# Turning mixing weights and normed head outputs by DMA transposes through memory instead of TensorE transposes

## The chip, the cores and the metric

The kernel runs on one core of one Trainium2 chip. The metric is the device time of one execution in microseconds (us), as a median of several runs. A profile of one execution gives, for the same program, the start and the duration of each instruction on each engine: TensorE (PE, its weight loads listed as PEld), VectorE (DVE), ScalarE (ACT), GpSimd (POOL) and SyncE (SP). POOL, SP and ACT also issue DMAs; all DMAs run on the core's 16 DMA engines.

## The reference, cut to what matters

A two-layer backbone over 256 latent and 256 context tokens with model width 1024, so 512 tokens in all. Layer 0 mixes tokens with a bidirectional mLSTM of 4 heads (256 for q and k, 512 for v), layer 1 with latent attention; a gated convolutional FFN follows each. The change lies in the mLSTM mixer. The recurrence is written in the reference as a chunked scan:

```
wmat = jnp.exp(dmat - mj[..., None]) * jnp.einsum("bhjd,bhsd->bhjs", qc, kc)
num  = g[..., None] * jnp.einsum("bhjd,bhde->bhje", qc, C) + jnp.einsum("bhjs,bhse->bhje", wmat, vc)
h    = num / jnp.maximum(jnp.abs(den), jnp.exp(-mj))[..., None]
...
o    = jax.nn.sigmoid(h_in @ w_og).reshape(Bq, T, M_HEADS, M_DV)
hsum = o * s.transpose(0, 2, 1, 3).astype(h_in.dtype)
return _head_rms_norm(hsum, norm_g) @ w_out
```

For each head and direction a token j thus takes a weighted sum of the values of the tokens s that it may see, divided by the row's own sum; the two directions are added, the result is gated by `o`, normed per token and head, scaled by a gain per column and multiplied by `w_out` (2048 x 1024).

## The kernel before, in words

All matrix products work on f32 numbers that are split into a high part and a low remainder (`split`, lines 443 to 445: ACT copies the high part, DVE subtracts for the low one), and each product is three matmuls (`mm3`, lines 424 to 434: high by high at L430, high by low at L433, low by high at L434). A weight block of 128 x 1024 comes by a DMA on SP's queue (L308) into a ring of raw buffers, is cast by ACT (L345) and subtracted by DVE (L368), and lies in one of three `w` buffers until PE has used it. `Stream` runs up to 8 blocks ahead, as far as buffers are free.

The mLSTM is not run as a scan: for each head the whole 512-token matrix of mixing weights is built, and multiplied with the values. Tokens lie in four tiles of 128 rows, t = 0 and 1 context, t = 2 and 3 latent. Context rows see columns 0 to 255, latent rows columns 0 to 511. The stages for head h are:

- `w_qk(h)`: q and k of head h by 8 chunks of 24 matmuls on one weight block each (L430, L433, L434, named `qk`). After each chunk `tick(2)` puts two steps of the generators in `k.bg` into the program, first the first generator's steps until it is used up, then the next one's. This is how the head before is worked on beside these matmuls: `post(h-2)`, then `head(h-1)`. Ahead of chunk 7 `v_load(h-1)` is put in: four loads of values (`vr`, L1133) and four of output gates (`oh`, L1139) on POOL's queue.
- `head(h-1)`: ACT makes the exponentials, DVE multiplies them by the scores S and normalises, in three groups g: context tiles 0 and 1 together, tile 2, tile 3; the last DVE instruction of a group is L1105. What comes out is rows of mixing weights, tokens j on partitions. The product with the values needs them the other way round, so TensorE turns the 12 blocks of 128 x 128 that are not masked (L1118, twelve `PT<-ident,W` in three PSUM tiles), and ACT and DVE split them from PSUM (L444, L445).
- `av(h-1)`: 36 matmuls of mixing weights by values; DVE multiplies the result by the gate into the tiles `oh` (L1178).
- `s_mm(h)`: scores of head h.
- `post(h-2)`: ACT squares and sums each of the four `oh` tiles (L1188), DVE scales them (L1192), TensorE turns them by 16 transposes of 128 x 128 (L1198, `hnT<-ident,oh`), and ACT and DVE read PSUM, apply the gain per column (which after turning is one number per partition) and split (L1205, L1206) into `hn[4h]` to `hn[4h+3]`.

After `w_qk(3)`, `av(2)` and `s_mm(3)` comes the product with `w_out` (`outmm("mout", ...)`, PE rows named `y`, one weight block and 12 matmuls for each of 16 steps i, of which step i needs `hn[i]`), first for the context tokens. Steps 0 to 7 run with `k.bg = [head(3), post(2)]`, then `av(3)`, then steps 8 to 11, which need `hn[8]` to `hn[11]` of head 2, beside `post(3)`, then steps 12 to 15. Head 3's own transposes stay on TensorE after the change too (`big`, `last`).

Names that matter for space: tag `s2`, 15 buffers of 128 x 512 f32 that nearly all small tiles of these stages share; tag `u`, 31 buffers of 128 x 1024 for split operands. A tile's buffer is given on when the last instruction that touches the tile is done, and a later tile with that tag waits for one. The order of instructions on each engine is made by the framework's scheduler: program order is the priority, and an instruction whose inputs are late lets later ones past it when the program is built, not when it runs. On the chip each queue is worked off strictly in that order.

Of the kernel before, what the change touches and what calls it, by code (L numbers as in the profile page):

```python
# [7 lines left out]
F32 = mybir.dt.float32  # L8
F32R = mybir.dt.float32r
I32 = mybir.dt.int32  # L10
AF = mybir.ActivationFunctionType
ALU = mybir.AluOpType
AX = mybir.AxisListType
# [20 lines left out]
NB, NRAW, NU, NS = 3, 3, 31, 15  # L34
# [366 lines left out]
class K:  # L401
# [41 lines left out]
    def split(self, hi, lo, src):  # L443
        self.nc.scalar.copy(hi, src)  # L444
        self.nc.vector.tensor_sub(lo, src, hi)  # L445

    def smc(self, name):
        o, n = self.off[name]
# [590 lines left out]
        return S  # L1039

    def head(self, h, S, big=False):
        nc = self.nc
        aB = [self.s2("aB0"), self.s2("aB1")]
        for d in range(2):
            nc.gpsimd.dma_start(aB[d], self.ad[d, h:h + 1, :].to_broadcast([128, 512]))
        if not big:
            self.t4_step(2)
        Am = [self.s2("Am0"), self.s2("Am1")]
        for d in range(2):
            nc.vector.tensor_tensor(Am[d].rearrange("p (t s) -> p t s", t=4),  # L1050
                                    aB[d].rearrange("p (t s) -> p t s", t=4),
                                    self.mask[:, d:d + 1, :].to_broadcast([128, 4, 128]), op=ALU.add)
        yield
        full = {0: [(0, 0), (0, 128), (0, 256), (0, 384)], 1: [(128, 256), (0, 0), (0, 256), (0, 256)]}
        P = []
        for g in range(3):
            jbs = [0, 1] if g == 0 else [g + 1]
            if big:
                w = self.uf("W")
                W = [w[:, 0:512], w[:, 512:1024]]  # L1060
            else:
                W = [self.s2("W0"), self.s2("W1")]
            den = self.tiny(4, "den")
            nd = len(jbs)
            rng = {}
            for i, t in enumerate(jbs):
                base = 256 * i if g == 0 else 0
                for d in range(2):
                    o = W[d]
                    bias = self.gcol[:, 0, t, 32 * d + h:32 * d + h + 1]  # L1070
                    spans = [(t * 128, (t + 1) * 128, Am[d])]
                    if d == 0:
                        if t > 0:
                            spans.append((0, t * 128, aB[d]))
                        lo, hi = 0, (t + 1) * 128
                    else:
                        if t == 0:
                            spans.append((128, 256, aB[d]))
                        if t >= 2:
                            spans.append((0, 256, aB[d]))  # L1080
                        if t == 2:
                            spans.append((384, 512, aB[d]))
                        lo, hi = {0: (0, 256), 1: (128, 256), 2: (0, 512), 3: (0, 512)}[t]
                    if d == 1 and t == 3:
                        nc.vector.memset(o[:, 256:384], 0.0)
                    for s0, s1, src in spans:
                        nc.scalar.activation(o[:, base + s0:base + s1], src[:, s0:s1], AF.Exp, bias=bias, scale=1.0)
                    nc.vector.scalar_tensor_tensor(o[:, base + lo:base + hi], o[:, base + lo:base + hi], 1.0,
                                                   S[g][:, base + lo:base + hi], op0=ALU.mult, op1=ALU.mult,
                                                   accum_out=den[:, 2 * i + d:2 * i + d + 1])  # L1090
                    rng[i, d] = (base + lo, base + hi)
            dv = den[:, 0:2 * nd]
            R = self.tiny(4, "R")
            nc.vector.scalar_tensor_tensor(R[:, 0:2 * nd], dv, -1.0, dv, op0=ALU.mult, op1=ALU.max)
            e = self.gcol[:, 1, jbs[0]:jbs[-1] + 1, h::32]
            nc.vector.tensor_tensor(R[:, 0:2 * nd].rearrange("p (t d) -> p t d", d=2),
                                    R[:, 0:2 * nd].rearrange("p (t d) -> p t d", d=2), e, op=ALU.max)
            nc.vector.reciprocal(R[:, 0:2 * nd], R[:, 0:2 * nd])
            for i, t in enumerate(jbs):
                big = {0: 1, 1: 0, 2: 1, 3: 0}[t]  # L1100
                b0, b1 = rng[i, big]
                s0, s1 = rng[i, 1 - big]
                nc.vector.tensor_scalar(W[big][:, b0:b1], W[big][:, b0:b1], R[:, 2 * i + big:2 * i + big + 1], None,
                                        op0=ALU.mult)
                nc.vector.scalar_tensor_tensor(W[big][:, s0:s1], W[1 - big][:, s0:s1],  # L1105
                                               R[:, 2 * i + 1 - big:2 * i + 2 - big], W[big][:, s0:s1],
                                               op0=ALU.mult, op1=ALU.add)
                P.append((W[big], b0))
            yield
        yield  # L1110
        self.PT = []
        for grp in ([(t, s) for s in range(2) for t in (0, 1)], [(t, s) for s in range(2) for t in (2, 3)],
                    [(t, s) for s in (2, 3) for t in (2, 3)]):
            pt = self.ps("PT")
            lead = None
            for n, (t, s) in sorted(enumerate(grp), key=lambda x: -x[1][0] * (x[1][0] > 1)):
                src, b0 = P[t]
                q = nc.tensor.transpose(pt[:, n * 128:(n + 1) * 128], src[:, b0 + s * 128:b0 + (s + 1) * 128], self.ident)  # L1118
                if lead is None:
                    lead = q  # L1120
                elif t > 1:
                    self.behind(q, [lead])
            u = self.u("PT")
            self.split(u[:, 0], u[:, 1], pt)
            self.PT.append(u)
        yield
# [53 lines left out]
        self.PT = self.vh = self.oh = None  # L1180
        return r

    def post(self, h, tt):
        nc = self.nc
        ss = self.tiny(4, "ss")
        jk = self.s2("jk")
# [4 lines left out]
        for t in range(4):  # L1191
            nc.vector.tensor_scalar(tt[t], tt[t], ss[:, t:t + 1], None, op0=ALU.mult)  # L1192
        yield
        g = self.smc("mng")
        for e in range(4):
            pt = self.ps("hnT")
# [6 lines left out]
            k = h * 4 + e  # L1203
            u = self.u("hn")
            nc.scalar.activation(u[:, 0], pt, AF.Copy, scale=g[:, k:k + 1])  # L1205
            nc.vector.scalar_tensor_tensor(u[:, 1], pt, g[:, k:k + 1], u[:, 0], op0=ALU.mult, op1=ALU.subtract)  # L1206
            self.hn[k] = u
        yield


    def bcast(self, row, name):
# [970 lines left out]
def build(tc, off, a, out):  # L2182
    es = ExitStack()
    with es:
# [14 lines left out]
        k.bg2.append(k.ada_all([(0, 3, 4, 8)] + [(l, c, 0, 8) for l, c in ((0, 4), (0, 5), (1, 0), (1, 1), (1, 2), (1, 3), (1, 4), (1, 5))]))  # L2199
        S = None  # L2200
        tt = None
        k.hn = {}
        for h in range(H0):
            gens = []
            if h == 0:
# [2 lines left out]
                gens.append(k.post(h - 2, tt))  # L2208
            if h >= 1:
                gens.append(k.head(h - 1, S))  # L2210
            k.bg = gens
            k.w_qk(h, 2, (lambda: k.v_load(h - 1)) if h >= 1 else None)
            k.drain()
# [3 lines left out]
        k.xc = None  # L2217
        hn = lambda i: (k.hn[i][:, 0], k.hn[i][:, 1])
        pc = k.acc4()
        k.bg = [k.head(3, S, True), k.post(2, tt)]  # L2220
        vs = k.v_steps(3)
        for i in range(8):
            k.outmm("mout", range(i, i + 1), hn, pc, 0, 16, 2, n2=ADA_M)
            next(vs, None)
        k.drain()
        tt = k.av(3)
        k.bg = [k.post(3, tt)]
        k.outmm("mout", range(8, 12), hn, pc, 0, 16, 1, n2=ADA_M)
        k.drain()
        tokr = a["tok"].rearrange("(t p) d -> t p d", p=128)  # L2230
# [132 lines left out]
```

## Time and profile before

| what | value |
|---|---|
| median of 3 runs | 1346.94 us (1346.42 to 1347.75) |
| span of the profiled execution, first to last instruction | 1345.3 us |
| median minus that span (the page gives no other time of the profiled execution) | 1.6 us |
| VectorE busy | 1059.0 us (79%) |
| ScalarE busy | 711.7 us (53%) |
| GpSimd busy | 141.5 us (11%) |
| moved by DMA | 304.02 MB, mean 226 GB/s |

Starts are given in us from the span's start. "busy (x)" in a table of stages is busy time and number of instructions in that stretch. A row of the timeline has start, duration, engine, line, operation, output and inputs, shape, and a count where equal neighbours were merged. A matmul's duration is its whole way through the array; the next one starts before it has ended, so what a matmul costs is read from the distance of starts. DMA issues are listed with the queue that issues them, size, and the median time from issue to landing.

### The profile page before, as it was taken

What the parts mean: (1) busy time and instruction counts of PE and PEld (TensorE: products, weight loads), DVE (VectorE), ACT (ScalarE), POOL (GpSimd) and SP (SyncE); (2) the same over time, 40 slices, a digit from 0 to 9 for tenths busy, and PEclk for the clock granted to TensorE, in tenths of its full rate; (3) what the DMA queues carried; (4) which work ended last, traced back from release to release, by engine and by line L of the source; (5) the groups of instructions that cost most, each with busy time, mean ns of one, the idle gap of its engine ahead of it and who ended that gap; (6) DMA issues with size and microseconds to landing.
All of it is one profiled execution on the core that took longest, in us unless ns stands there. A gap on an engine that the chain in (4) does not pass through costs nothing.

```text
span 1345.3 us, 18750 instructions
## 1 busy us (share of the span) xinstructions
PE 1334.9 (99%) x6659; PEld 1120.2 (83%) x6659; DVE 1059.0 (79%) x1745; ACT 711.7 (53%) x1252; POOL 141.5 (11%) x236
## 2 busy tenths in 40 slices
PE   9999999999999999999999999999999999999997
PEld 5777888888888888888898888888888998988886
DVE  4798656678688696897979977758899889898874
ACT  4765444445744546474644334333566767676660
POOL 0222000011101011020002011111000002000100
PEclk9999999999999999999999999999999999999999
DMA  9988848889686384776628989967866437376750
GB/s 364 330 277 279 281 163 248 233 272 307 235 281 230 102 255 149 228 292 222 215 86 261 328 260 286 282 181 184 300 223 194 157 104 219 127 212 189 263 189 32
DMA packets 99885, 304.02 MB, mean 226 GB/s; under 512 B 12312, under 2 KB 25112, under 8 KB 99712
## 3 DMA queue, kind: packets, MB, share of 16 engines
q1 hardware_dynamic: 62992, 218.65, 48.6%
q0 software_dynamic: 26000, 66.75, 17.9%
q10 hardware_dynamic: 10800, 17.44, 3.6%
q8 instruction: 52, 0.85, 0.3%
q14 instruction: 41, 0.34, 0.1%
HBM read 272.21 MB, written 42.12 MB: 234 GB/s over the span
## 4 chain that ended last, share of the span: by engine, by line
PE 97%; DMA 1%; DVE 1%; ACT 0%; issue 0%; SPq 0%; DVEq 0%; ACTq 0%
PE fin L1503 8%; PE tok L430 6%; PE tok L434 6%; PE tok L433 6%; PE fin L433 6%; PE fin L434 6%; PE y L433 6%; PE fin L430 6%; PE y L434 6%; PE y L430 6%; PE qk L430 4%; PE qk L433 4%; PE qk L434 4%; PE up L718 2%; PE up L430 2%; PE up L434 1%
## 5 line engine op out<-in xcount | busy, mean ns | idle before, releaser
L368 DVE TENSOR_TENSOR w<-raw,w 128x1024 fp32r<-128x1024 f32 (+2 forms) x286 | 343.2, 1203 | 131.9 <-ACT w L345 129.7
L345 ACT CAST w<-raw 128x1024 fp32r<-128x1024 f32 (+2 forms) x286 | 296.2, 1037 | 282.4 <-PE tok L434 77.8
L544 DVE SCALAR_TENSOR_TENSOR junk<-ar,bc 128x1024 f32<-128x1024 f32 x128 | 156.1, 1219 | 5.2 <-ACT bc L586 2.3
L433 PE MATMUL fin<-h,w 128*128 128x512 f32 (+1 forms) x370 | 139.6, 377 | 0.0
L430 PE MATMUL fin<-h,w 128*128 128x512 f32 (+1 forms) x370 | 139.5, 377 | 0.0
L434 PE MATMUL fin<-h,w 128*128 128x512 f32 (+1 forms) x370 | 139.3, 377 | 0.0
L1503 PE MATMUL fin<-h,w 128*128 128x512 f32 (+1 forms) x636 | 111.1, 337 | 0.0
L1503 PEld LDWEIGHTS fin<-h,w 128*128 128x128 f32 x636 | 97.6, 190 | 13.2
L430 PE MATMUL qk<-xc,w 128*128 128x512 f32 x256 | 100.2, 391 | 0.0
L434 PE MATMUL qk<-xc,w 128*128 128x512 f32 x256 | 99.8, 390 | 0.0
L433 PE MATMUL qk<-xc,w 128*128 128x512 f32 x256 | 99.6, 389 | 0.0
L433 PEld LDWEIGHTS fin<-h,w 128*128 128x128 f32 x370 | 69.6, 188 | 13.0
L430 PEld LDWEIGHTS fin<-h,w 128*128 128x128 f32 x370 | 69.6, 188 | 12.9
L434 PEld LDWEIGHTS fin<-h,w 128*128 128x128 f32 x370 | 69.6, 188 | 12.6
L434 PEld LDWEIGHTS qk<-xc,w 128*128 128x128 f32 x256 | 48.0, 188 | 10.1
L430 PEld LDWEIGHTS qk<-xc,w 128*128 128x128 f32 x256 | 48.1, 188 | 9.8
L433 PEld LDWEIGHTS qk<-xc,w 128*128 128x128 f32 x256 | 48.1, 188 | 9.8
L430 PE MATMUL tok<-w,hT 128*128 128x512 f32 x128 | 49.9, 390 | 0.0
L433 PE MATMUL tok<-w,hT 128*128 128x512 f32 x128 | 49.8, 389 | 0.0
L434 PE MATMUL tok<-w,hT 128*128 128x512 f32 x128 | 49.8, 389 | 0.0
L735 ACT ACTIVATE fg<-fg 128x512 f32<-128x512 f32 (+1 forms) x44 | 23.1, 525 | 50.0 <-DVE fg L733 43.9
L368 DVE TENSOR_TENSOR wu<-raw,wu 128x1024 fp32r<-128x1024 f32 (+1 forms) x37 | 43.8, 1203 | 3.5 <-ACT wu L345 3.2
(486 smaller groups left out, 3125.7 us busy)
## 6 DMA issues: line engine op xcount, KB each, us to landing
raw<-in_ws SPq DMA_DIRECT2D x282, 512.0 KB, 4.5
ar<-in_adaT SPq DMA_DIRECT2D x80, 512.0 KB, 6.0
t4d<-in_ws POOLq DMA_DIRECT2D x20, 512.0 KB, 9.1
adaw<-in_ada SPq DMA_DIRECT2D x16, 512.0 KB, 8.0
zr<-fd ACTq DMA_DIRECT2D x33, 128.0 KB, 4.6
xmd<-xr POOLq DMA_DIRECT2D x16, 256.0 KB, 4.4
xcd<-cv POOLq DMA_DIRECT2D x16, 256.0 KB, 4.9
xs<-xmd POOLq DMA_DIRECT2D x16, 256.0 KB, 6.0
```

The source lines that it names most:

```text
L345: self.cast = k.nc.scalar.copy(h[:, :cols], src)
L368: i = self.k.nc.vector.tensor_sub(l[:, :n], src, h[:, :n])
L430: q = mm(out, w[0], x[0], start=start, stop=False, skip_group_check=on)
L433: mm(out, w[0], x[1], start=False, stop=False, skip_group_check=on)
L434: mm(out, w[1], x[0], start=False, stop=stop, skip_group_check=on)
L544: nc.vector.scalar_tensor_tensor(o, w, 1.0, self.bc[j], op0=ALU.mult, op1=ALU.mult, accum_out=col[:, k, j:j + 1])
L718: nc.tensor.matmul(ps[m], wk[i][:, c], hT[k][:, j], start=made[m] == 0, stop=made[m] == 23)
L735: nc.scalar.activation(tmp[:, :n], tmp[:, :n], AF.Silu)
L1503: self.nc.tensor.matmul(ps[:, 0:256] if x else ps, w[x][:, k * 128:(k + 1) * 128], h[:, 0:256] if x else h, start=i == 0 and not k0, stop= ...
```

## The change

For heads 0, 1 and 2 both kinds of TensorE transposes are replaced. A tile of f32 rows is copied by ACT into two planes of 16-bit halves (`planes`), stored to a scratch tensor in memory by a DMA on POOL's queue, and read back by a transposing DMA on SP's queue (`dma_start_transpose`, 2-byte elements), so that the two halves of each number come to lie next to each other again, with partitions and tokens exchanged. The splits into high and low parts then read these tiles in SBUF and not PSUM. In `head` three transposing DMAs of 512 rows x 256 columns replace 12 TensorE transposes; in `post` four stores and, in the new generator `turn_heads`, four transposing DMAs of 1024 rows x 128 columns replace 16. `turn_heads` stands behind `post` and `head` in `k.bg`.

```diff
+    def planes(self, dst, src):
+
+        i = self.nc.scalar.copy(dst, src.bitcast(U16).rearrange("p (n h) -> p h n", h=2))
+        return i
...
     def head(self, h, S, big=False):
-        nc = self.nc
+        nc, last = self.nc, big
+        pd = None if last else self.dr.tile([512, 2, 512], U16, name="pd")
...
                 P.append((W[big], b0))
+            if not last:
+                n = 256 if g == 0 else 512
+                pl = self.pool.tile([128, 2, 512], U16, tag="s2", name="pl", bufs=NS)
+                for i, t in enumerate(jbs):
+                    p = pl if g else pl.rearrange("p a (b n) -> p (a b) n", b=2)[:, 2 * i:2 * i + 2]
+                    src, b0 = P[t]
+                    self.planes(p, src[:, b0:b0 + n])
+                    nc.gpsimd.dma_start(pd[t * 128:(t + 1) * 128, :, 0:n], p)
             yield
         yield
         self.PT = []
+        if not last:
+            v = pd.rearrange("t h n -> (t h) n")
+            for t0, s0 in ((0, 0), (2, 0), (2, 2)):
+                x = self.s2("px")
+                nc.sync.dma_start_transpose(x.bitcast(U16).rearrange("p (s t) -> p s t", s=2),
+                                            v[256 * t0:256 * t0 + 512, 128 * s0:128 * s0 + 256])
+                u = self.u("PT")
+                self.split(u[:, 0], u[:, 1], x)
+                self.PT.append(u)
+            yield
+            return
...
-    def post(self, h, tt):
+    def post(self, h, tt, last=False):
...
         yield
+        if not last:
+            d = self.dr.tile([512, 2, 512], U16, name="hd")
+            for t in range(4):
+                pl = self.pool.tile([128, 2, 512], U16, tag="s2", name="pl", bufs=NS)
+                self.planes(pl, tt[t])
+                nc.gpsimd.dma_start(d[t * 128:(t + 1) * 128], pl)
+            self.turned.append((h, d))
+            yield
+            return
...
+    def turn_heads(self):
+
+        nc, g = self.nc, self.smc("mng")
+        h, d = self.turned.pop(0)
+        v = d.rearrange("t h n -> (t h) n")
+        xs = []
+        for e in range(4):
+            x = self.s2("hx")
+            nc.sync.dma_start_transpose(x.bitcast(U16), v[:, e * 128:(e + 1) * 128])
+            xs.append(x)
+            if e % 2:
+                yield
+        for e in range(4):
+            k, x = h * 4 + e, xs[e]
+            u = self.u("hn")
+            nc.scalar.activation(u[:, 0], x, AF.Copy, scale=g[:, k:k + 1])
+            nc.vector.scalar_tensor_tensor(u[:, 1], x, g[:, k:k + 1], u[:, 0], op0=ALU.mult, op1=ALU.subtract)
+            self.hn[k] = u
+            xs[e] = x = None
+            if e % 2:
+                yield
...
             if h >= 1:
                 gens.append(k.head(h - 1, S))
+            if h >= 2:
+                gens.append(k.turn_heads())
...
-        k.bg = [k.head(3, S, True), k.post(2, tt)]
+        k.bg = [k.head(3, S, True), k.post(2, tt), k.turn_heads()]
...
-        k.bg = [k.post(3, tt)]
+        k.bg = [k.post(3, tt, True)]
```

More of the change, by code (lines that the diff above doesn't have):

```diff
@@ L10 @@
 I32 = mybir.dt.int32
+U16 = mybir.dt.uint16
 AF = mybir.ActivationFunctionType
@@ L2201, in build @@
         tt = None
-        k.hn = {}
+        k.hn, k.turned = {}, []
         for h in range(H0):
```

## The prediction

> **What bounds the kernel now.** I read the page first, then the table of stages, then the instructions by tile, and last the timeline around each transpose.
>
> ```profile
> PE 1334.9 (99%) x6659; PEld 1120.2 (83%) x6659; DVE 1059.0 (79%) x1745; ACT 711.7 (53%) x1252; POOL 141.5 (11%) x236
> PE 97%; DMA 1%; DVE 1%; ACT 0%; issue 0%; SPq 0%; DVEq 0%; ACTq 0%
> ```
>
> The first line is the busy time of the engines, the second the chain that ended last. PE is busy for 99% of the span and is 97% of that chain, so PE time that is taken away shortens the kernel one for one, as long as nothing that PE needs comes late. The same must hold in the stages that the change touches: 459.40 to 504.00 is `w_qk(2)`, 577.50 to 601.50 steps 0 to 7 of the output product, 601.50 to 610.00 `av(3)`.
>
> ```profile
> core 0: us, PE busy (x) PEld busy (x) DVE busy (x) ACT busy (x) POOL busy (x), PEclk, DMA share, GB/s
> 459.40:504.00 44.60, 44.60 (x212) 37.05 (x211) 39.08 (x82) 26.08 (x58) 6.42 (x12) 1.00 0.67 207
> 577.50:601.50 24.00, 24.00 (x121) 20.02 (x120) 22.20 (x60) 18.17 (x41) 7.61 (x15) 1.00 0.72 260
> 601.50:610.00 8.50, 8.50 (x40) 7.00 (x38) 5.44 (x9) 3.55 (x9) 1.61 (x3) 1.00 0.82 312
> ```
>
> PE has no gap in any of them and the granted clock is 1.00. DVE is the next bound (39.08 of 44.60 us, 22.20 of 24.00); ACT and the DMA engines have room.
>
> **What is removed.** By tile, the two kinds of transposes are:
>
> ```profile
> L1118 PE MATMUL PT<-ident,W x48: 270/272/298, 417.3 to 595.6; 128*128 128x128 f32 x48
> L1198 PE MATMUL hnT<-ident,oh x64: 270/273/328, 465.1 to 616.9; 128*128 128x128 f32 x64
> ```
>
> That is 12 and 16 for each of four heads; three heads lose theirs, so 36 and 48 go. The 272 ns are the way through the array, not the price. The price is how far a group pushes two ordinary matmuls apart. Undisturbed, matmuls follow each other as here, in `av(3)`:
>
> ```profile
> 602.29 0.39 PE L430 MATMUL av<-v,PT 128*128 128x512 f32 x1
> 609.77 0.39 PE L430 MATMUL y<-w,hn 128*128 128x512 f32 x1
> ```
>
> Between the two starts lie 33 matmuls: 7.48 / 33 = 0.227 us each. Now a group of twelve (head 2), one of sixteen (head 0) and the sixteen of head 2:
>
> ```profile
> 546.34 0.39 PE L434 MATMUL qk<-xc,w 128*128 128x512 f32 x1
> 546.57 1.47 PE L1118 MATMUL PT<-ident,W 128*128 128x128 f32 x12
> 547.80 0.47 PE L430 MATMUL qk<-xc,w 128*128 128x512 f32 x1
> 548.12 0.39 PE L433 MATMUL qk<-xc,w 128*128 128x512 f32 x1
> ...
> 464.77 0.39 PE L434 MATMUL qk<-xc,w 128*128 128x512 f32 x1
> 465.06 2.03 PE L1198 MATMUL hnT<-ident,oh 128*128 128x128 f32 x16
> 467.17 0.40 PE L433 MATMUL qk<-xc,w 128*128 128x512 f32 x1
> ...
> 598.23 0.39 PE L434 MATMUL y<-w,hn 128*128 128x512 f32 x1
> 598.46 1.91 PE L1198 MATMUL hnT<-ident,oh 128*128 128x128 f32 x16
> 600.44 0.39 PE L433 MATMUL y<-w,hn 128*128 128x512 f32 x1
> ```
>
> From the matmul before to the second one behind there would be 2 x 0.227 = 0.454 us without the group. So twelve cost 548.12 - 546.34 - 0.454 = 1.33 us, head 0's sixteen 467.17 - 464.77 - 0.454 = 1.95, head 2's 600.44 - 598.23 - 0.454 = 1.76. Taking head 1 like head 0 for the sixteen and head 2 for the twelve of all three heads, the sum is 3 x 1.33 + 2 x 1.95 + 1.76 = **9.64 us**, or 0.11 us a transpose. It is the whole of what can be won.
>
> **What is added, beside PE.** These rows price it: a cast of 128 x 1024 for a plane copy, the two operations that follow a turn, and DMAs with their median times from issue to landing.
>
> ```profile
> L345 ACT CAST w<-raw 128x1024 fp32r<-128x1024 f32 (+2 forms) x286 | 296.2, 1037 | 282.4 <-PE tok L434 77.8
> ...
> L1205 ACT ACTIVATE hn<-hnT,sm x16: 674/684/700, 466.0 to 618.1; 128x512 fp32r<-128x512 f32 x16
> L1206 DVE SCALAR_TENSOR_TENSOR hn<-hnT,sm,hn x16: 741/743/751, 467.3 to 619.6; 128x512 fp32r<-128x512 f32 x16
> ...
> xmd<-xr POOLq DMA_DIRECT2D x16, 256.0 KB, 4.4
> xcd<-cv POOLq DMA_DIRECT2D x16, 256.0 KB, 4.9
> vd<-v POOLq DMA_DIRECT2D x16, 256.0 KB, 6.7
> x3d<-z POOLq DMA_DIRECT2D x4, 256.0 KB, 2.3
> raw<-in_ws SPq DMA_DIRECT2D x6, 256.0 KB, 4.2
> out_dram<-z SPq DMA_DIRECT2D x2, 256.0 KB, 2.0
> t4d<-in_ws POOLq DMA_DIRECT2D x20, 512.0 KB, 9.1
> ```
>
> *ACT.* For each head six copies of 1024 16-bit elements per partition (1.04 us) and two of 512 (0.69 at most): 7.6 us. In `w_qk(2)` ACT would have 33.7 us of work in 44.60 - 3.28 = 41.3 us (3.28 being the 1.95 and 1.33 that leave this stage). It holds. *DVE* gets no instruction and loses none, but 39.08 us must fit into 41.3: 2.2 us of room are left there, and should DVE take 5% longer PE would wait for weight splits.
>
> *POOL's queue.* Seven stores for each head. Each waits for its copy, and behind it wait the loads of `vr` and `oh`, of `aB` and, for head 2, `xres` and `gate`.
>
> *SP's queue.* Seven transposing DMAs for each head wait until the stores have landed, and the weight loads (L308) wait behind them on SP.
>
> ```profile
> 578.16 14.61 SPq L308 DMA_DIRECT2D raw<-in_ws  x3
> 604.13 12.66 SPq L308 DMA_DIRECT2D raw<-in_ws  x5
> ```
>
> Around head 2's turn no weight is loaded from 592.8 to 604.1, because the ring is full, and five follow. A step of the output product uses a block in 12 x 0.227 = 2.72 us and six raw buffers are in the ring then, some 16 us of cover. Held until 606.4 (below), SP would issue four DMAs and come to its weight loads some 4 us late. I cost it at nothing; without the cover it is those 4 us.
>
> *Mixing weights of heads 0 to 2.* Take head 1, whose cover is among the smaller:
>
> ```profile
> 484.79 0.74 DVE L1105 SCALAR_TENSOR_TENSOR W<-W,R 128x512 f32<-128x512 f32 x1
> 505.05 0.39 PE L430 MATMUL av<-v,PT 128*128 128x512 f32 x1
> ```
>
> The weights are done at 485.5, the plane copy at 486.6, the store has landed at 491.2 (4.65, between the two commonest 256 KB stores of POOL), the first transposing DMA at 495.4 (4.2, SP's 256 KB load), the split is done 0.69 + 0.74 = 1.43 us later, at 496.9. `av(1)` then begins at 505.05 - 3.28 = 501.8. 4.9 us of cover: nothing lost.
>
> *Head 2's normed output* is where I expect a wait. Its gain is fixed by PE's arrival at step 8: 609.77 - 1.76 = 608.0. The chain starts here:
>
> ```profile
> 596.43 1.15 ACT L444 CAST v<-vr 128x512 fp32r<-128x512 f32 x2
> 597.38 1.26 DVE L1192 TENSOR_SCALAR oh<-oh,ss 128x512 f32<-128x512 f32 x3
> ```
>
> DVE, not PE, sets these times, so they stay. ACT is free at 597.6, four copies of 1.04 end at 601.7; the last store lands at 601.7 + 4.65 = 606.4; `turn_heads` needs all four stores for every one of its DMAs; the first lands at 610.6; ACT and DVE make `hn[8]` by 612.0. PE waits 612.0 - 608.0 = **4.0 us**, and nothing else is there for it: steps 12 to 15 need head 3, and `post(3)` comes later. The next three `hn` have 2.72 us each, so they cost nothing if the DMAs land at least that close together. The bounds: with the quickest rows (2.3 and 2.0) `hn[8]` is there at 607.5 and nothing is lost; with the slowest (6.7 and 9.1) at 619.0, and 11.0 us are. I take the middle because its rows are 256 KB transfers on these very queues.
>
> No row of this kernel shows a transposing DMA, and two rules of the Trainium skill differ on it. "DMA: Bandwidth & Descriptors", section Latency and other measured facts, gives 261 GB/s for a transposing DMA, by which 256 KB would take an estimated 1.0 us and the sum above stands. "VectorE: DVE Perf Modes", section The three transpose paths, gives 1309 ns for a 128 x 128 block of 2-byte elements on the DMA crossbar and 390 ns on TensorE; by it a DMA of eight blocks would take an estimated 10.5 us and the change would lose. No run here shows the first figure; the second page's 390 ns is far from the 0.11 us that a transpose costs PE above.
>
> **Sum.** -9.64 + 4.0 = -5.6 us. The profiled span is 1345.3 us, 1.6 below the median of 1346.94; what lies outside the span does not change, so the median becomes 1346.94 - 5.6 = **1341.3**. Its own range is 1337.3 (no wait) to 1348.3 (11.0 us).
>
> **Rivals.** *Everything is covered* (stores and turns as quick as the quickest rows): 1346.94 - 9.64 = 1337.3. For it: DMA share is 0.46 to 0.82 and PE hides all else. Against it: two transfers through memory in a row within 6.3 us. Chance 0.15.
>
> *The transposing DMAs are slow, one after the other.* If they land y us apart, the four of `turn_heads` cost 4.0 + 3(y - 2.72) us. It decides from y = 4.6 (all won is lost) and is measurably slower from 5.5. At y = 9.1, the slowest landing quoted, the first `hn` is 4.9 us later still, 28 in all, and mixing weights of heads 1 and 2 come at 491.2 + 3 x 9.1 + 1.4 = 519.9 against 505.9, where `av` first needs the third tile (501.8 and 18 matmuls of 0.227): 14 us each. 28 + 28 - 9.6 = 46 slower, 1393. For it: no row shows at what rate 16-bit elements are turned. Against: landing times include a wait in queues, and 256 KB loads need not be 4 us apart. Chance 0.12. By the second page's 10.5 us this rival would give some 1407.
>
> *The `s2` buffers run out.* A head's stage takes 22 of them before (1 `jk`, 4 `aB` and `Am`, 6 `W`, 4 `vr`, 4 `oh`, 3 `S`) and 36 after (7 `pl`, 3 `px`, 4 `hx` more), with 15 to go round. The values' loads stood far ahead:
>
> ```profile
> 467.18 1.65 POOL L1133 DMA_DIRECT2D vr<-vd  x3 [43.37 <-PE hnT L1198]
> ...
> vr<-vd POOLq DMA_DIRECT2D x16, 256.0 KB, 4.7
> ```
>
> They are already bound by such a buffer (43.37 us of waiting for `hnT`). Loaded from s on, `v` is there at s + 4.7 + 1.43; `av(1)` waits for it from s = 495.7, all is lost from 498.5 (2.8 us each in heads 1 and 2), and it is measurably slower from 499.9. If they wait for `turn_heads` to its end at the end of `w_qk(2)`, 501.8, it is 2 x 6.1 us: 1346.94 - 9.64 + 4.0 + 12.2 = 1353.5. Against it: when the last group's copies are done at 486.6, only `gcol`, one `pl`, three `px` and four `hx` are held, and six buffers are free. Chance 0.10.
>
> **How the numbers follow.** Likeliest case 0.55, the three rivals 0.37, another order of some queue 0.08. A measurement here can tell 0.2%, 2.7 us, from no change. The likeliest case is faster by more than that if the wait is under 6.9 us: 0.45 of its 0.55; with the first rival 0.15 and 0.02 of the rest, faster is 0.62. Within 0.2% lie 0.07 of the likeliest case, and mild forms of the others, 0.15 in all; slower 0.23. The range from 1337.0 to 1351.0 holds the likeliest case and the first rival, and leaves out the slow crossbar and the worst of the buffers.
>
> **What would show it.** Right: the 48 transposes into `PT` and 64 into `hnT` shrink to 12 and 16; PE has one new gap, of 2 to 7 us, ahead of step 8 (`y`, about 600 us from the start), released by DVE's low part of `hn` behind a DMA; `av` of heads 0 to 2 starts without one; transposing DMAs land within 2.7 us of each other. Wrong: gaps ahead of `av(1)` and `av(2)`; several gaps between steps 8 and 11; PE waiting for `w` behind a late weight load; or DVE at 100% in `w_qk(2)`.

## The result, and the profile after

The changed kernel takes 1388.15 us (median of 5 runs, 1385.94 to 1390.49) against 1346.92 us of the kernel before in the same rounds: a ratio of 1.0308, 95% interval 1.0295 to 1.0320. It is 41 us slower, where 1341.3 us was forecast and the range ended at 1351. The profiled execution has a span of 1388.7 us, 43.4 more than before.

The page of the changed kernel: busy times, the chain that ended last, and the first DMA queues (packets, MB, share of 16 engines).

```profile
PE 1333.9 (96%) x6575; PEld 1114.9 (80%) x6575; DVE 1058.9 (76%) x1745; ACT 733.7 (53%) x1276; POOL 155.4 (11%) x260
...
q1 hardware_dynamic: 85168, 224.16, 49.6%
q0 software_dynamic: 27728, 72.25, 18.5%
...
PE 82%; issue 11%; DMA 3%; POOL 1%; DVE 1%; ACT 1%; SPq 0%; DVEq 0%; POOLq 0%
```

PE has 84 matmuls fewer (6659 - 6575), as the change says, and is off the chain for 18% of the span. SP's queue (q1) has 22,176 packets more than the 62,992 that the page of before counts, for 5.5 MB more: some 250 bytes each. These are the transposing DMAs.

What PE waited for, as total, times and longest, in the changed kernel:

```profile
PE av L431 <- ACT v L445: 27.1, 2, 14.0
PE y L431 <- ACT hn L1260: 16.0, 1, 16.0
PE av L434 <- DVE v L446: 1.6, 2, 1.4
```

Before, none of these rows exists. The stretches around the third gap, as in the table of stages (PEclk and DMA share are the columns before the last):

```profile
630.00:635.00 5.00, 4.66 (x17) 2.96 (x17) 4.17 (x6) 0.79 (x3) 4.15 (x8) 1.00 0.96 295
635.00:640.00 5.00, 0.00 (x0) 0.00 (x0) 0.00 (x0) 0.00 (x0) 1.97 (x4) 0.89 1.10 296
640.00:645.00 5.00, 0.00 (x0) 0.00 (x0) 0.00 (x0) 0.00 (x0) 0.18 (x1) 0.50 1.10 256
...
650.00:655.00 5.00, 4.29 (x10) 3.42 (x11) 2.03 (x3) 3.28 (x7) 0.79 (x2) 0.50 1.17 181
655.00:660.00 5.00, 5.00 (x21) 4.06 (x21) 3.07 (x5) 2.81 (x5) 0.28 (x1) 0.90 0.17 56
```

While PE stands, the granted clock falls to 0.50, and it is still there when PE starts again: ten matmuls from 650.71 to 655, where 0.227 us for each would make it 19. So each of these three gaps costs its own length and then some 2 us. `av(1)`'s 36 matmuls, for example, take 11.63 us against 8.16 in the kernel before, and 1.4 of the difference is a wait. The account, an estimate, is then 27.1 + 1.6 + 16.0 of waits, less the forecast 9.64 removed, 35.1; three times some 2 us of half clock, about 41; and some 2 us of the 43.4 that I can't place.

The way to `av(1)` in the changed kernel, from the timeline:

```profile
466.43 0.54 POOL L1225 DMA_DIRECT2D hd<-pl  x1 [0.41 <-ACT pl L450]
467.25 0.54 POOL L1052 DMA_DIRECT2D aB<-ad  x1 [0.27 <-issue]
...
496.04 0.75 DVE L1112 SCALAR_TENSOR_TENSOR W<-W,R 128x512 f32<-128x512 f32 x1
...
498.99 2.24 POOL L1159 DMA_DIRECT2D vr<-vd  x4 [0.29 <-issue]
...
502.76 5.92 SPq L1131 DMA_TRANSPOSE px<-pd  x2
...
510.44 0.62 ACT L445 CAST PT<-px 128x512 fp32r<-128x512 f32 x1 [8.62 <-DMA px<-pd]
...
513.70 2.17 ACT L445 CAST v<-vr 128x512 fp32r<-128x512 f32 x4
514.36 0.80 PE L431 MATMUL av<-v,PT 128*128 128x512 f32 x1 [13.13 <-ACT v L445]
```

Three things are late here. The loads of `aB`, with which the mixing weights begin, stand on POOL's queue behind the new `hd` stores, at 467.25; before, head 1's first was issued at

```profile
418.19 0.54 POOL L1045 DMA_DIRECT2D aB<-ad  x1 [7.19 <-DVE junk L544]
```

so the mixing weights are done at 496.8 and not at 485.5. The pair of transposing DMAs issued at 502.76 is first used at 510.44. And the values, issued at 498.99, 0.8 us after the last plane store and without a wait for a buffer, are cast behind that on ACT's queue. Ahead of step 8:

```profile
629.91 2.19 POOL L1623 DMA_DIRECT2D xres<-in_tok  x4 [0.17 <-issue]
631.97 20.52 SPq L1253 DMA_TRANSPOSE hx<-hd  x4
...
649.94 0.72 ACT L1260 ACTIVATE hn<-hx,sm 128x512 fp32r<-128x512 f32 x1 [19.15 <-DMA hx<-hd]
...
650.71 0.80 PE L431 MATMUL y<-w,hn 128*128 128x512 f32 x1 [16.04 <-ACT hn L1260]
```

The first of the four was forecast to land 4.2 us after its issue. It was first used after 18.0. The four issues held SP's queue for 20.5 us.

### The profile page after: what moved, and what is told of

Its sections match the earlier page's. It is cut to its first block, busy times and chain, and to the rows that moved or that the text cites. A ratio compares the mean times of both kernels' runs of the same rounds, so it can differ in the third digit from the quotient of the medians.

```text
span 1388.7 us, 18708 instructions
## 1 busy us (share of the span) xinstructions
PE 1333.9 (96%) x6575; PEld 1114.9 (80%) x6575; DVE 1058.9 (76%) x1745; ACT 733.7 (53%) x1276; POOL 155.4 (11%) x260
## 4 chain that ended last, share of the span: by engine, by line
PE 82%; issue 11%; DMA 3%; POOL 1%; DVE 1%; ACT 1%; SPq 0%; DVEq 0%; POOLq 0%
PE fin L1560 8%; PE tok L431 6%; PE tok L435 6%; PE tok L434 6%; PE fin L435 6%; PE fin L431 6%; PE fin L434 6%; PE y L431 6%; PE y L434 6%; PE y L435 6%; PE up L724 2%; PE up L431 1%; PE up L435 1%; PE up L434 1%; PE y L1403 1%
## 5 line engine op out<-in xcount | busy, mean ns | idle before, releaser
L431 PE MATMUL y<-w,hn 128*128 128x512 f32 x92 | 36.8, 405 | 16.0 <-ACT hn L1260 16.0
```

The costliest lines, as they stand in the source:

```text
L431: q = mm(out, w[0], x[0], start=start, stop=False, skip_group_check=on)
```

## The experiments

The theory had three parts, with the letters of the texts that were written ahead of the runs: **A**, a transposing DMA is quick alone but starves while POOL's queue loads; **C**, the order on POOL's queue makes the mixing weights late; **D**, the values come late, by their place in the queues of loads and casts. Its rivals: **B**, the transposing DMAs are slow by themselves, or `s2` buffers are short. All results in one table, waits of PE in us; the kernel before, timed beside each, took 1346.9 to 1347.5. The changed kernel's time and those with a ratio and its interval are medians of 4 to 10 executions, the others are single executions; waits are those of one profiled execution. In the four kernels that change nothing ahead of `av` but buffers (changed, hn2_pe, xres_late, after_s17) the waits at `av` lie between 28.7 and 33.8, so differences of 5 us there say nothing.

| kernel | time, us | waits at av | at step 8 | others |
|---|---|---|---|---|
| changed | 1388.15 | 28.7 | 16.0 | |
| pt_only | 1362.12 | 13.7 | none | |
| hn_only | 1370.14 | none | 14.4 | PT 8.3 |
| hn2_pe | 1377.84 | 32.6 | none | |
| xres_late | 1384.82 | 31.8 | 5.3 | sc 1.4 |
| ab_early | 1381.76 | 20.2 | 15.1 | sc 1.4 |
| split_late | 1372.06 | 6.8 | none | 16 in the output product's stage |
| v_early | 1372.06 (1.0185, 1.0170 to 1.0199) | 13.1 | 0.9 | sc 4.9 |
| v_on_sp | 1364.62 | 18.8 | none | hnT 1.7 |
| raw_first | 1372.68 (1.0193, 1.0178 to 1.0208) | 29.5 | none | |
| raw_first_late | 1369.71 (1.0164, 1.0147 to 1.0181) | 15.7 | none | PT 4.5, hnT 3.1 |
| vr_ahead | 1361.82 (1.0112, 1.0094 to 1.0130) | 6.3 | none | sc 5.2, hnT 1.3 |
| vr_between | 1360.00 | 5.8 | none | sc 3.3, hnT 2.4 |
| after_s17 | 1408.82 | 33.8 | 19.0 | tok 3.6, hnT 2.2 |
| early_ab | 1344.28 (0.9979, 0.9969 to 0.9988) | none | none | |

All these kernels but early_ab took longer than the theory that each was to test had forecast, by 4 to 30 us. So what the runs support are the places of the waits and what moves them; the sizes came out larger each time, in part because new waits came up elsewhere.

**The parts alone.** pt_only turns only the mixing weights by DMA, hn_only only the normed outputs, hn2_pe all but head 2's normed output; the cores of their diffs in this order:

```diff
-                gens.append(k.post(h - 2, tt))
+                gens.append(k.post(h - 2, tt, True))
...
-        nc, last = self.nc, big
+        nc, last = self.nc, True
...
-        k.bg = [k.head(3, S, True), k.post(2, tt), k.turn_heads()]
+        k.bg = [k.head(3, S, True), k.post(2, tt, True)]
```

> Only the mixing weights of heads 0 to 2 are turned by DMA, the normed outputs by TensorE as before. Theory A: no wait ahead of step 8, but the turned weights still land beside the loads of values and gates on POOL's queue, so av(1) and av(2) wait some 5 us each: 1346.9 - 4.0 + 10 + 3 for the lower clock behind a gap, about 1356. Theory C (the two av waits come from the aB loads, which stand behind the stores of normed outputs on POOL's queue, so that the weights are finished 11 us later): without these stores aB is early again and the waits go: about 1343 to 1346. Theory B: as A, with waits of 8 us and more.

> Only the normed outputs of heads 0 to 2 are turned by DMA, the mixing weights by TensorE as before. All theories: no wait ahead of av for want of turned weights; the wait ahead of step 8 stays, 12 to 16 us, with about 2 us of lower clock behind it: 1346.9 - 5.7 + 14 to 18, so 1355 to 1359. Theory C adds: aB is still late here, but with TensorE's turns there is cover enough for it.

> As the changed kernel, but head 2's normed output is turned by TensorE again. All theories: the wait ahead of step 8 (16 us and about 2 us of lower clock) goes, 1.8 us of transposes come back, the waits ahead of av(1) and av(2) stay at 13 to 14 us each: 1388 - 18 + 2 = about 1372.

Each part alone is slower. pt_only was expected at about 1356 by A and at 1346 or less by C; hn2_pe at 1372. hn_only was expected at 1355 to 1359 and came out at 1370: besides the gap ahead of step 8, its TensorE transposes of mixing weights wait,

```profile
PE PT L1144 <- DVE W L1112: 8.3, 2, 4.5
```

though no transposing DMA stands between the weights and PE there. That is C by itself: the `hd` stores ahead of `aB`. In early_ab (below) the same stores for heads 0 and 1 stay, TensorE turns the same weights of heads 1 and 2, `aB` is early, and this wait is gone. In pt_only no `hd` store exists and the waits at `av` are half as long. In hn2_pe the wait ahead of step 8 is gone and those at `av` stay (31.2 behind ACT's casts of `v`).

**The transposing DMA by itself.** The first small kernel let all its tiles share one buffer, so that its stages ran one transfer after the other and told only the time of one DMA.

> The kernel leaves out the whole computation: it holds only four transposing DMAs of 256 KB (1024 rows x 128 columns of 16 bits) in five stages: alone, alone again, beside ten 256 KB loads on POOL's queue, behind ten such loads on SP's own queue, and beside ten loads on POOL's queue of half the size in 256-byte pieces. Theory A (packets take turns: a transposing DMA moves 256-byte packets, and beside the 4096-byte packets of another queue it gets one for one): alone about 1.2 us apart, 5 us for four; beside POOL's loads 3 to 10 us apart until these loads are done; behind SP's loads again 1.2 us apart; beside 256-byte pieces about 2.5 us apart. Theory B (a transposing DMA is slow by itself): 5 to 6 us apart in every stage.

It took 194.92 us, with a transposing DMA of 256 KB every 3.6 us or so, each waiting for the one before. The second gave each tile its own buffer. Its stages turn the same four blocks alone, alone again, beside ten 256 KB loads on POOL's queue, behind ten such loads on SP's own, and beside loads in 256-byte pieces on POOL's.

```diff
+        stage(0, 0, nc.gpsimd)
+        stage(1, 0, nc.gpsimd)
+        stage(2, 10, nc.gpsimd)
+        stage(3, 10, nc.sync)
+        stage(4, 10, nc.gpsimd, True)
```

> As xbar_micro, which leaves out the whole computation, but each of the tiles has a buffer of its own, so that the four transposing DMAs of a stage and its loads are in flight together. Theory A (packets of 256 bytes beside packets of 4096 bytes of another queue get a small part of each DMA engine): alone the four land in some 7 us from the first issue (2 us and four times 1.2); beside ten 256 KB loads on POOL's queue they land only when these are nearly done, 12 us or more from the issue; behind ten loads on SP's own queue they take 1.2 us each once the loads are through; beside 256-byte pieces some 10 us. Theory B (slow by itself): 20 us and more in every stage.

Its DVE rows, one for each landing, in the order alone (first issue at 6.75), beside POOL's loads (which begin at 23.15; transposes from 23.49), behind SP's own (transposes from 52.62):

```profile
10.52 0.16 DVE L43 TENSOR_TENSOR mark<-hx,mark 128x1 f32<-128x1 f32 x1 [7.82 <-DMA hx<-hd]
12.06 0.16 DVE L43 TENSOR_TENSOR mark<-hx,mark 128x1 f32<-128x1 f32 x1 [1.39 <-DMA hx<-hd]
13.60 0.16 DVE L43 TENSOR_TENSOR mark<-hx,mark 128x1 f32<-128x1 f32 x1 [1.38 <-DMA hx<-hd]
14.60 0.16 DVE L43 TENSOR_TENSOR mark<-hx,mark 128x1 f32<-128x1 f32 x1 [0.83 <-DMA hx<-hd]
...
29.44 0.16 DVE L43 TENSOR_TENSOR mark<-hx,mark 128x1 f32<-128x1 f32 x1 [5.79 <-DMA hx<-hd]
42.27 0.16 DVE L43 TENSOR_TENSOR mark<-hx,mark 128x1 f32<-128x1 f32 x1 [12.68 <-DMA hx<-hd]
...
59.21 0.16 DVE L43 TENSOR_TENSOR mark<-hx,mark 128x1 f32<-128x1 f32 x1 [12.09 <-DMA hx<-hd]
60.57 0.16 DVE L43 TENSOR_TENSOR mark<-hx,mark 128x1 f32<-128x1 f32 x1 [1.20 <-DMA hx<-hd]
```

Alone, the first lands 3.8 us after its issue and the others 1.0 to 1.5 apart. Behind ten loads on the same queue, which are still under way, the first takes 6.6 us, and the others again come 1.1 to 1.4 apart. Beside POOL's loads the second lands 12.8 us after the first. A holds, and the rival that the transposing DMA is slow by itself falls. Beside loads in 256-byte pieces (of full size, not of half) the four took 16.7 us from the first issue, where A had some 10; but the trace has these loads in packets of 4096 bytes too, so that stage does not test what the size of a packet does.

**A in place.** xres_late keeps the loads of `xres`, and the `gate` loads behind them on POOL's queue, from starting before `hn[11]` is made, by one small copy into each tile that needs it.

```diff
+                if hold is not None:
+                    self.nc.scalar.copy(x[0:1, 0:1], hold)
```

> As the changed kernel, but the eight loads of xres on POOL's queue, which need nothing and ran beside head 2's four transposing DMAs, are held until hn[11] is made (one extra 1 x 1 copy on ACT for each). Theory A: with eight of some sixteen loads gone the DMAs of head 2 land earlier, the wait ahead of step 8 falls from 16 us to 6 to 9: about 1380. Theory B: the wait stays at 16 us, 1388.

The wait ahead of step 8 fell from 16.0 to 5.3, below the 6 to 9 expected; the first of the four was used 6.7 us after its issue and not 18.0. The total fell by only 3.3 us, since the waits at `av` behind casts of `v` were 30.4 in this execution.

```profile
PE av L431 <- ACT v L445: 30.4, 2, 17.0
PE y L431 <- ACT hn L1260: 5.3, 1, 5.3
```

**C in place.** ab_early issues the loads of `aB` for head h-1 ahead of `post(h-2)`.

```diff
+            k.aB = k.load_aB(h - 1) if h >= 2 else None
```

> As the changed kernel, but the two aB loads of a head stand ahead of the stores of normed outputs in the program. Theory C (half of each av wait is the lateness of aB): mixing weights are done some 7 to 10 us earlier in heads 1 and 2, the waits ahead of av(1) and av(2) fall from 13 to 14 us to 6 or 7 each, as with the mixing weights alone: 1388 - 14 = 1374. Theory A alone: no change, 1388.

The waits behind casts of `v` fell from 27.1 to 18.9, in the direction of C but short of the 12 to 14 expected. Head 1's mixing weights are done at 489.7 here,

```profile
488.93 0.74 DVE L1118 SCALAR_TENSOR_TENSOR W<-W,R 128x512 f32<-128x512 f32 x1
```

so 7.1 of the 11.3 us come back by the place of `aB` alone.

**D: the order of splits and values.** The next kernels all have early `aB` and head 2's normed output on TensorE. split_late puts the splits of `px` four steps later, behind the casts of values; v_early puts the loads and casts of values five chunks earlier; v_on_sp issues `vr` and `oh` on SP's queue. In this order:

```diff
+                px.append(x)
+            for _ in range(4):
+                yield
+            for x in px:
...
-VE = {1: (3, 0), 2: (3, 0), 3: (3, 0)}
+VE = {1: (1, 0), 2: (1, 0), 3: (1, 0)}
...
-            nc.gpsimd.dma_start(r, self.vd[h, s])
+            nc.sync.dma_start(r, self.vd[h, s])
```

> As ab_early with head 2's normed output on TensorE, and the splits of the turned mixing weights stand behind the casts of the values in ACT's and DVE's queues (four empty steps ahead of them). Theory D (part of the av wait is order: on ACT the casts of the values, which have landed, stand behind the splits, which wait for a DMA): the first six matmuls of av can start, the waits ahead of av(1) and av(2) fall from 9 us each by about 3: 1381.8 - 17 + 1.8 - 6 = about 1361. Theory A alone: the turned weights are as late as before and the waits stay at 9: about 1366.

> As ab_early with head 2's normed output on TensorE, and v_load (eight loads on POOL's queue and the casts of the values) stands five chunks earlier in the program, so that no load of POOL runs beside the transposing DMAs of the mixing weights and no cast of values stands behind their splits. Theory A with C and D: no wait ahead of av(1) and av(2) is left, or one of 1 us at most, and 7.9 us of transposes are saved: 1339 to 1342. Theory B (transposing DMAs are slow by themselves): waits of 5 us and more remain, 1350 or more.

> The kernel with a(B) loaded early and head 2's normed output turned on TensorE, whose values and gates (vr, oh) are loaded by SyncE's queue and not by GpSimd's. Theory (what is left of av's waits, 18.9 us with early aB, comes from the values' loads: on GpSimd's queue they stand behind the stores of the planes, ScalarE's casts of them stand ahead of nothing else, and their 4096-byte packets run beside the 256-byte ones of the transposing DMAs): av waits 0 to 6 us in all and the time is 1340 to 1350 us. Rival 1 (only the engines' turns by packets matter, whichever queue issues the loads): the px DMAs still land 8 us or more after their issue, av waits 10 us or more, and the time is 1355 to 1366. Rival 2 (SyncE's queue becomes the bound: weight loads stand behind loads of values and transposing DMAs): TensorE waits for w in the same stages, and the time is above 1366.

In split_late the waits at `av` fell to 6.8, but 16 us of new ones came up around the output product (5.9 for a weight block, 5.8 for head 3's mixing weights, 2.5 for `oh`). That fits the four steps having pushed other work back; no run separates it. v_early missed by 30 us. Its casts of `v` stand on ACT ahead of head 1's exponentials and wait there for loads, the last until 482.6, so that the exponentials begin at 484.5 and the mixing weights end at 502.2. v_on_sp left 18.8 us, as ab_early had, but for another reason: `px` was turned early and only the values were late, on SP behind `px` and `hx`. Its time lies in the range of rival 1, whose reason did not come: `px` is quick. Its SP and ACT rows:

```profile
495.50 2.58 SPq L1137 DMA_TRANSPOSE px<-pd  x2
498.16 0.53 SPq L309 DMA_DIRECT2D raw<-in_ws  x1
498.82 7.14 SPq L1259 DMA_TRANSPOSE hx<-hd  x4
506.07 1.93 SPq L1165 DMA_DIRECT2D vr<-vd  x4
```

```profile
499.37 0.62 ACT L446 CAST PT<-px 128x512 fp32r<-128x512 f32 x1 [3.35 <-DMA px<-pd]
...
510.01 1.26 ACT L446 CAST v<-vr 128x512 fp32r<-128x512 f32 x2 [7.24 <-DMA vr<-vd]
```

This is A once more, at `px`: with no load of POOL beside it the pair's first is used 3.9 us after its issue (4.5 and 3.7 in heads 0 and 2). With POOL's loads beside it, in ab_early, the same place reads 8.7 (11.5 and 12.3 in heads 0 and 2):

```profile
497.92 4.79 SPq L1137 DMA_TRANSPOSE px<-pd  x2
```

```profile
506.61 0.62 ACT L446 CAST PT<-px 128x512 fp32r<-128x512 f32 x1 [8.66 <-DMA px<-pd]
```

raw_first loads `vr` on POOL's queue ahead of the first chunk, casts left where they were; raw_first_late adds split_late's order. vr_ahead and vr_between are v_on_sp with the loads of `vr` two chunks and one chunk earlier on SP's queue. RAW, the pair of column block and half ahead of which the loads stand, is (0, 0), (0, 0), (2, 0) and (2, 1).

```diff
+                if early is not None and (j, c) == RAW:
+                    self.v_raw(h - 1)
```

> Early aB, head 2's normed output on TensorE, and the loads of values (vr) ahead of the first chunk of w_qk, in front of the stores of planes on GpSimd's queue; their casts stay where they are in ScalarE's queue, behind the splits of px. Theory (av's waits have three parts: late aB, the transposing DMAs of px that run beside the loads of vr, and the values that are late themselves): both the second and the third part are much less, so av waits 0 to 6 us in all and the time is 1339 to 1347 us. Rival (the transposing DMAs of px are slow whatever else runs, or the gates' loads are enough to hold them up): px still lands 8 us after its issue, av waits 10 us or more, 1355 to 1366.

> As raw_first, and the splits of px stand behind the casts of values in ScalarE's queue. By the theory the values are split while the transposing DMAs run, so that only the splits of px are left between the landing and av: 0 to 3 us of waits at av, 1339 to 1345 us. By the rival as raw_first: 1355 or more. A third outcome is open, that the later steps of head() push other work of the stage back, as when the splits alone were moved: waits of hnT, PT and y in the output product's stage, 1350 to 1370.

> As v_on_sp (early aB, head 2's normed output on TensorE, values and gates by SyncE's queue), with the loads of values alone put into the program two chunks earlier, so that on SyncE's queue they stand ahead of the transposing DMAs of px and not behind px and hx. Theory (in v_on_sp px was turned by 501.0 and only the values were late; the transposing DMAs are quick when GpSimd's queue loads nothing beside them): av waits 0 to 4 us in all and the time is 1340 to 1350 us. Rival (something else of the stage, such as the splits on ScalarE or weight loads held up by SyncE, sets av's start): waits of 8 us or more ahead of av, or new ones for w, and 1356 or more.

> As vr_ahead, one chunk later: on SyncE's queue the values stand behind px and ahead of hx. Theory: the values come some 5 us after px, so av waits about 2 to 5 us each time, 4 to 10 us in all, 1344 to 1356 us. Rival: as vr_ahead, 1356 or more.

raw_first doesn't decide it: `av(0)` waits there too, the plane stores of `post(0)` begin at 472.9 and head 1's weights are copied at 500.4, and the gates' loads still run beside `px` (issued 507.02, first used 516.16). raw_first_late ends between the two theories, again with new waits at the output product (`PT` 4.5, `hnT` 3.1). vr_ahead and vr_between do: 18.8 becomes 6.3 and 5.8, by the place of four loads alone. So the three parts A, C and D together make most of the waits at `av`; what makes the last 6 us was not looked into. The times, 1362 and 1360, are above what the theory forecast and where its rival had them (1356 or more), though neither of the rival's reasons came: no 8 us at `av`, no wait for `w`. The first reason is new waits, for scores above all (5.2 in vr_ahead). The longest, 4.4 us ahead of `sc` at 584.6, fits A again: the fourth `hx` was issued at 568.59, beside `aB` loads on POOL's queue, and first used at 577.69; DVE stood 6.0 us for its `hn`, with the split of `qk` that the scores need behind it.

```profile
577.69 0.72 ACT L1276 ACTIVATE hn<-hx,sm 128x512 fp32r<-128x512 f32 x1 [5.09 <-DMA hx<-hd]
578.45 0.75 DVE L1277 SCALAR_TENSOR_TENSOR hn<-hx,sm,hn 128x512 fp32r<-128x512 f32 x1 [6.00 <-ACT hn L1276]
```

The second reason stands in vr_ahead's table of stages around its 3.1 us gap ahead of `av(1)`:

```profile
500.00:504.00 4.00, 0.90 (x4) 0.40 (x3) 2.82 (x4) 2.28 (x5) 0.00 (x0) 0.99 1.08 230
504.00:508.00 4.00, 3.86 (x10) 2.73 (x11) 3.95 (x7) 2.96 (x5) 1.08 (x2) 0.58 1.34 202
508.00:512.00 4.00, 4.00 (x19) 3.31 (x18) 0.90 (x2) 1.66 (x2) 0.00 (x0) 1.00 1.06 79
```

Even a gap of 3 us is followed by half clock: 10 matmuls in 4 us, at 0.58. The waits in vr_ahead are 12.8 us, 7.9 are removed by the prediction's prices, and the span is 13.3 us longer than before, so some 8.4 us are left. Most of that is the slow start: after the three gaps of 3.1, 3.2 and 4.4 us PE ran 3.3, 5.8 and 4.7 us at half clock, and half of that, 6.9 us, is lost. After the gap of 1.25 us ahead of `hnT` the clock stayed at 1.00.

**Buffers.** after_s17 is the changed kernel with two `s2` buffers more and one of `u` less.

```diff
-NB, NRAW, NU, NS = 3, 3, 31, 15
+NB, NRAW, NU, NS = 3, 3, 30, 17
```

> The changed kernel with 17 small buffers (tag s2) instead of 15, paid for with one of the 31 buffers of tag u. Theory (the order of instructions in the queues of GpSimd, ScalarE and the DMA engines makes the waits; buffers are not short): TensorE's waits stay as they are, some 27 us ahead of av(1) and av(2) and 16 us ahead of step 8, and the time is 1385 to 1391 us. Rival (the prediction's third: the 36 small tiles of a stage find too few buffers, so loads and copies start late): with two more the waits of av fall by a third or more, to 18 us or less, and the time to 1378 or below.

The waits didn't shrink, and head 1's `aB` loads came behind the `hd` stores as in the changed kernel (473.58). It is 20 us slower, with some small waits elsewhere; how much of that is the missing `u` buffer was not measured. Nothing here speaks for short `s2` buffers as the cause, but as two tags changed at once, and the time met neither forecast, the run does not rule them out; that the changed kernel's loads of `vr` followed the plane stores without a wait speaks against them.

**What is worth keeping.** early_ab turns by DMA only what has cover: the mixing weights of head 0 and the normed outputs of heads 0 and 1, with early `aB`.

```diff
-        nc, last = self.nc, big
+        nc, last = self.nc, h > 0
...
-        k.bg = [k.head(3, S, True), k.post(2, tt), k.turn_heads()]
+        k.bg = [k.head(3, S, True), k.post(2, tt, True)]
```

> A version meant to beat both: turned by DMA are only those tiles that have time, the mixing weights of head 0 and the normed outputs of heads 0 and 1; the rest is turned by TensorE, and aB is loaded ahead of the stores. All theories: 1.33 + 2 x 1.95 = 5.2 us of transposes go, and no wait takes their place: about 1341.7. If theory A also slows what is late elsewhere (loads of values, weights), up to 1347.

Its PE has no wait that before hadn't:

```profile
PE idle L662 <- DVE adav L504: 1.5, 1, 1.5
PE up L725 <- DVE hT L700: 0.3, 1, 0.3
```

By the prediction's prices 1.33 + 2 x 1.95 = 5.2 us are removed. From the first matmul of `w_qk(0)` to the first of `av(3)`, where all of these transposes stood, PE needs 4.5 us less than before (352.21 to 597.04 against 352.28 to 601.59). The median fell by 2.9 us: 0.21% faster than the kernel before. The profiled execution was the quickest of ten, so its span (1341.1 against 1345.3) overstates the gain; where the rest of the 5.2 went is not shown. Head 0's pair of `px` lands late here too (issued 428.20, used 437.82), but `av(0)` comes late enough not to feel it.

## Why the prediction was wrong, point by point

- **What is removed** was right in number, 84 transposes, and nearly so in price: 4.5 of 5.2 us in early_ab's stages, of which the median kept 2.9.
- **"The first lands at 610.6 (4.2, SP's 256 KB load)"** is the step that failed for head 2. The row was a plain load (SP's queue before: 218.65 MB in 62,992 packets, some 3.5 KB each); the new DMA moves 256 KB in packets of some 250 bytes, with POOL's loads of `oh`, `xres` and `gate` beside it. 4.2 became 18.0 us, and 4.0 us of wait 16.0. With `xres` and `gate` held back the wait was 5.3. The waits at `av`, 28.7 of the 44.7 us in all, come from the next two steps. The prediction did list `xres` and `gate`, but only as queued behind the stores, not as running beside the turn.
- **"The weights are done at 485.5"** failed next. It took this time from before, though the paragraph on POOL's queue had said that `aB` stands behind the stores. What stands behind a store that waits for a copy is late by that wait; it was priced at nothing. The weights came 11.3 us later, against 4.9 us of cover, and 7.1 of these came back with `aB` early. Its next step, 4.2 us from issue to landing for `px`, was short as well: the pair was first used after 7.7.
- **The values** were in the third rival, with the right price (a wait from an issue at 495.7 on; it was 498.99) and the wrong cause: order in the queues and not buffers.
- **The chance** of 0.12 for slow transposing DMAs, 1393 us, lies close to what was measured, but not for its reason: they don't land y us apart whatever else runs. That the two numbers lie close is chance. The pace of at most 2.72 us apart was right when they have the engines to themselves (1.0 to 1.5).
- **Not in the sum at all:** the half clock after each of the three gaps, about 2 us a gap.
- **Right as well:** no wait for weight blocks in the changed kernel, none at `av(0)`, DVE below its bound, plane copies at 1.05 us. The signs named as "wrong", gaps ahead of `av(1)` and `av(2)`, are those that came.

## What to carry to other kernels

Work taken from a busy engine and put onto queues must be followed through each of these queues: list for each instruction that is now behind the new ones when it was issued before, and take that wait as a price, not the median landing. The duration of a transfer is a statement about what ran beside it; for a DMA in small packets, look up which loads of other queues fall into its stretch. And where PE is busy for 99% of the span, move only those parts whose cover is longer than the slowest landing: a part of this change wins 0.2%, the whole loses 3%.

## What the runs showed of the hardware

A transposing DMA of 256 KB lands 3.8 us after its issue, and further ones 1.0 to 1.5 us apart, about 170 to 260 GB/s. The issue of each holds SP's queue for 1.2 to 1.3 us, so this pace may be that of the issue as much as that of the transfer. Four of them beside 256 KB loads of another queue took some 20 us, and behind loads on their own queue 10.3 from the first issue, against 7.9 alone. While the changed kernel waits ahead of step 8, from 638 to 644 us, its trace has 341 packets of 4096 bytes on POOL's queue and 638 of at most 256 bytes on SP's: 1.4 MB against 0.16 MB. The Trainium skill ("DMA: Bandwidth & Descriptors", section Queues, rings and completion order) states that each DMA engine takes turns between queues packet by packet. That small packets lose by this fits, but is an inference: the runs here show the slowing and the packets' size, not the turns themselves. The 1309 ns for a block of 128 x 128 in "VectorE: DVE Perf Modes" of the Trainium skill, section The three transpose paths, don't hold for blocks in a row: eight blocks landed every 1.0 to 1.5 us.

In the changed kernel's three gaps the granted clock fell to 0.50, 4.0 to 4.9 us after the last matmul had begun, and PE then ran 3.3 to 5.3 us at half clock, with matmuls 0.43 us apart and not 0.227. In vr_ahead a gap of 3.1 us had the same effect and one of 1.25 us had none; in vr_between a wait of 2.1 us was followed by half clock, too. The Trainium skill ("TensorE: Matmul & The Clock Gate", section Part 1: The HAM clock gate) gives 426.7 ns and names an idle window of about 3.4 us. The distance agrees; the 2.1 us are shorter than that window.
